# Hybrid block on one core: the state space group's tiles rebuilt, and linear attention's products issued in turn

## The chip, the core and the metric

One NeuronCore of a Trainium2 chip runs the kernel alone. The metric is the device time of one execution in microseconds; the figure given for a kernel is the median of several runs. TensorE multiplies on an array of 128 rows by 128 columns: a product's contraction lies on the rows (the partitions of its operands), its stationary operand's columns on the array's columns. The profile gives the clock that was granted to TensorE as a share of 2.4 GHz.

## The reference

A diffusion block on 1024 latent tokens behind 256 context tokens (D = 1024): one input projection feeds three groups (RWKV-7 with 4 heads, Mamba-2 state space with 8 heads of 64 and 2 groups of state 64, gated linear attention with 4 heads), an output projection joins them, and a mixture of experts follows. Each group is scanned in both directions and the two results are added. The state space group works in chunks of 128 tokens:

```python
def ssd_chunked(x, dA, bm, cm, s0):          # x is already times dt
    a_cs = cumsum(dA over the chunk)
    decay_in = exp(where(causal, a_cs[l] - a_cs[s], -inf))
    scores = einsum('bclhn,bcshn->bhcls', cm, bm) * decay_in
    y_diag = einsum('bhcls,bcshp->bclhp', scores, x)
    decay_to_end = exp(a_cs[-1] - a_cs)
    states = einsum('bclhn,bhcl,bclhp->bchpn', bm, decay_to_end, x)
    states = running sum over chunks, each decayed by the chunks behind it
    y_off = einsum('bclhn,bchpn,bhcl->bclhp', cm, states[:, :-1], exp(a_cs))
    return y_diag + y_off
```

Linear attention (`gla_chunked`) has the same form in chunks of 64 tokens with keys of 32 and values of 64: masked scores by values, and decayed queries by the chunk's state. (The code above is condensed.)

## The kernel before

The sequence is 10 tiles of 128 tokens; tiles 0 and 1 are context and give only states. `block_kernel` emits, in order: the input projection and the setup of all groups (to 560 us), 20 steps of the RWKV scan (`rw_step`), `rw_finish`, `gla_states`, `ssd_dt`, `ssd_states`, `ssd_out` for tiles 2 to 5, `gla_out`, the loads for the output projection, `ssd_out` for tiles 6 to 9, the output projection, routing, and the experts. This is not the order in which they run: the tile framework builds a timeline of its own from the emitted program and sets each engine's order from it, so the work of several of these functions is interleaved. Every engine then runs its list strictly in order; nearly all DMAs are issued on one queue, SP, in order too. PSUM is divided while the scan and the groups run: 2 buffers for the scan (`ch`), 1 (`rg`), 3 for the state space group (`sd`) and 2 for linear attention (`gl`).

The state space group before, per tile:

- `ssd_consts2` (L941) writes a template `difD` to DRAM early; `ssd_dt` (L955) fills it, by 32 small DMAs (L1015, L1016), with the cumulative sums of dA, each split into three bf16 parts so that bf16 products add up to float32 accuracy.
- `ssd_states` (L1019): the tile's x and B are transposed (`ptx`, `ptB`), x is multiplied by the decay to the chunk's end (`xs`, once per direction), and `pss` (L1044) gives the tile's state, [64 of a group's state rows on 64 partitions, 256]. Then, per direction, a chain on GpSimd over the tiles (`sacc`, L1059 multiply and L1061 add, 128x256), whose values ScalarE copies into `g.st` in SBUF.
- `ssd_weights` (L1067): `pe` (L1079), one bf16 product on 44 rows for each direction and half of the heads, gives the difference of cumulative sums at every (source, target); ScalarE copies one direction, VectorE takes the minimum of both, ScalarE the exponential (`E`). `pcb` (L1088) is C by B; VectorE multiplies it by the two masks (`M`), ScalarE and VectorE apply dt per head (`G`, L1094, L1095), GpSimd multiplies `E` by `G` (L1097).
- `ssd_out` (L1101): `pyo` (L1116) is C by the state, 64 rows and 512 columns; VectorE scales it (L1120), GpSimd adds the directions (`yo`); in `pyd`, x by `E` (L1131, two heads on the two column halves) and a transpose of `yo` by the identity (L1132) add up; VectorE adds the skip term (L1135), GpSimd gates (L1137), and squares are summed for the norm.

`gla_out` (L866): for each head `pat` (L880, 32 rows, 64 columns, the two chunks of a tile on the column halves) gives scores; `po` (L902, L905) collects values by scores and states by queries, one buffer after the other. `inv_norm` (L363) spreads norm factors over partitions with a float32 product by the identity (`pbn`, L378).

Of the kernel before, what the change touches and what calls it, by code (L numbers as in the profile page):

```python
# [362 lines left out]
def inv_norm(g, W, tag, sq, blk, scale, eps):  # L363
# [502 lines left out]
def gla_out(g):  # L866

    nc = g.nc
    W = g.gl
    for gr in range(2):  # L870
        att = W.tile([128, 2 * TT], F, tag="la", name="att", bufs=1)
        asum = att[:, 0:1024].rearrange("p (h j t) -> p h j t", h=4, j=4)
        for h in range(4):
            hs = slice(32 * h, 32 * h + 32)
            ps = g.ps.tile([128, 2, 4, 64], F, tag="gl", name="pat")
            for d in range(2):
                for j in range(4):
                    for i in range(2):
                        c = slice(512 * gr + 128 * j + 64 * i, 512 * gr + 128 * j + 64 * i + 64)
                        nc.tensor.matmul(ps[HS[i], d, j, :], g.gq[d][hs, 1, c], g.gq[d][hs, 0, c], start=True,  # L880
                                         stop=True)
            at = att[:, 1024 + 512 * (h % 2):1536 + 512 * (h % 2)].rearrange("p (d j t) -> p d j t", d=2, j=4)
            nc.gpsimd.memset(at, 0.0)
            for d in range(2):
                nc.vector.copy_predicated(at[:, d], g.mA[:, d, None, :].to_broadcast([128, 4, 64]), ps[:, d])
            nc.vector.tensor_add(asum[:, h], at[:, 0], at[:, 1])
        oTs = []
        for hp in range(2):
            oT = W.tile([128, 512], F, tag="oT", name="oT", bufs=2)
            for i in range(2):  # L890
                po = g.ps.tile([128, 4, 64], F, tag="gl", name="po")

                for d in (-1, 0, 1):
                    for j in range(4):
                        tl = 2 + 4 * gr + j
                        c = 2 * tl + i
                        cs = slice(64 * c - TC, 64 * c - TC + 64)
                        for h in (2 * hp, 2 * hp + 1):
                            o = po[HS[h % 2], j, :]
# [7 lines left out]
                nc.scalar.activation(oT.rearrange("p (j i t) -> p j i t", i=2, t=64)[:, :, i, :], po, AF.Copy)  # L907
# [32 lines left out]

def ssd_consts2(g):  # L941


    nc = g.nc
    g.difD = g.dram.tile([8, 44, 4, 5, 128], BF, name="difD")
    t = g.tmp.tile([44, 4, 5, 128], BF, tag="rv", name="dift", bufs=1)
    nc.gpsimd.memset(t, 0.0)
    nc.gpsimd.memset(t[0:12, :, 0], 1.0)
    for h in range(4):
        nc.sync.dma_start(t[32 + 3 * h:35 + 3 * h, :, 1 + h], g.oneb[0:3, None, :].to_broadcast([3, 4, 128]))  # L950
    nc.sync.dma_start(g.difD.rearrange("c p i j t -> p c (i j t)"),
                      t.rearrange("p i j t -> p (i j t)")[:, None].to_broadcast([44, 8, 2560]))


def ssd_dt(g):  # L955

    nc, W = g.nc, g.sd
    n = 160
# [14 lines left out]
    m = W.tile([128, 160], I32, tag="srs", name="dm")  # L973
    nc.vector.tensor_scalar(m, f(u), 1.0 / 16, None, op0=OP.is_lt)
    nc.vector.copy_predicated(f(e), m, f(p))
    nc.vector.tensor_scalar(x, x, 0.0, None, op0=OP.max)
    g.dtp = T("dtp")
    nc.vector.tensor_add(g.dtp, x, e)
    dA = T("dA")
    for d in range(2):  # L980
        nc.vector.tensor_mul(dA[:, d], g.dtp[:, d], g.nea[:, d, None, :].to_broadcast([128, 10, 8]))
    g.eacs, g.wend = T("eacs"), T("wend")
    tot = T("tot")
    for d in range(2):
        ps = g.ps.tile([128, 4, 128], F, tag="sd", name="psd")
        r = dA[:, d].rearrange("p c h -> p (c h)")
        nc.tensor.matmul(ps[:, 0, 0:80], g.mT[:, d, :], r, start=True, stop=True)
        nc.tensor.matmul(ps[:, 1, 0:80], g.mT[:, 2 + d, :], r, start=True, stop=True)
        nc.tensor.matmul(ps[:, 2, 0:80], g.onesm, r, start=True, stop=True)
        for i, dst in ((0, g.eacs), (1, g.wend), (2, tot)):  # L990
            nc.scalar.activation(dst[:, d].rearrange("p c h -> p (c h)"), ps[:, i, 0:80], AF.Exp)
    nc.vector.tensor_mul(g.wend, g.wend, g.dtp)

    g.dec = W.tile([128, 2, 10, 4], F, tag="dec", name="dec")
    for h in range(2):
        nc.vector.tensor_copy(g.dec[HS[h]], tot[HS[h], :, :, 4 * h:4 * h + 4])

    ps = g.ps.tile([128, 512], F, tag="sd", name="pcs")
# [12 lines left out]
    for d in range(2):
        for q in range(2):
            for h in range(4):
                src = parts[64 * d + 4 * q + h:64 * d + 64:8]
                nc.sync.dma_start(g.difD[:, 3 * h:3 * h + 3, 2 * d + q, 1 + h], src[:, 0:3])  # L1015
                nc.sync.dma_start(g.difD[:, 32 + 3 * h:35 + 3 * h, 2 * d + q, 0], src[:, 3:6])  # L1016


def ssd_states(g):  # L1019
    nc, W = g.nc, g.sd  # L1020
    g.xr = g.dram.tile([10, 128, 512], F, tag="sxr", name="sxr")
    g.st = W.tile([128, 2, 8, 256], F, tag="st", name="st")
    sc = W.tile([128, 2, 2, 256], F, tag="E", name="sc", bufs=2)
    for tl in range(10):
# [21 lines left out]
        nc.vector.tensor_copy(sc[:, :, tl, :] if tl < 2 else g.st[:, :, tl - 2, :], ps)

    for d in range(2):
        order = list(range(10)) if d == 0 else [1, 0] + list(range(9, 1, -1))
        acc = None  # L1050
        for i, tl in enumerate(order):
            own = sc[:, d, tl, :] if tl < 2 else g.st[:, d, tl - 2, :]
            if i == 0:
                acc = W.tile([128, 256], F, tag="sacc", name="sacc", bufs=3)
                nc.gpsimd.tensor_copy(acc, own)
                continue
            if i < 9:
                nxt = W.tile([128, 256], F, tag="sacc", name="sacc", bufs=3)
                nc.gpsimd.tensor_mul(nxt.rearrange("p (h c) -> p h c", h=4), acc.rearrange("p (h c) -> p h c", h=4),  # L1059
                                     g.dec[:, d, tl, :, None].to_broadcast([128, 4, 64]))  # L1060
# [753 lines left out]
```

## Time and profile before

| | |
|---|---|
| median of 3 runs | 1552.88 us (1551.18 to 1554.76) |
| profiled execution | 1557.75 us, its span 1555.9 us |
| mean granted clock | 0.874 |
| TensorE busy in the span | 1363.9 us (88%) |
| VectorE / ScalarE / GpSimd busy | 816.0 / 522.8 / 401.2 us |
| instructions | 28009 |

The span is the time between the first and the last record of the profiled execution; the rest of its time lies around it. A busy share over the whole span mixes stages that have different limits, so the stages are read apart: the projection to about 560 us, the RWKV scan to 730, what is left of the states to 780, the products of the state space group and of linear attention to 930, the output projection to 1057, routing to 1105, experts to the end. "Idle before" in a group names what the engine waited for last.

### The profile page before, as it was taken

What the parts mean: (1) busy time and instruction counts of PE and PEld (TensorE: products, weight loads), DVE (VectorE), ACT (ScalarE), POOL (GpSimd) and SP (SyncE); (2) the same over time, 40 slices, a digit from 0 to 9 for tenths busy, and PEclk for the clock granted to TensorE, in tenths of its full rate; (3) what the DMA queues carried; (4) which work ended last, traced back from release to release, by engine and by line L of the source; (5) the groups of instructions that cost most, each with busy time, mean ns of one, the idle gap of its engine ahead of it and who ended that gap; (6) DMA issues with size and microseconds to landing.
All of it is one profiled execution on the core that took longest, in us unless ns stands there. A gap on an engine that the chain in (4) does not pass through costs nothing. (4 is left out here: it accounts for less than half of the span.)

```text
span 1555.9 us, 28009 instructions
## 1 busy us (share of the span) xinstructions
PE 1363.9 (88%) x11016; PEld 1122.0 (72%) x11016; DVE 816.0 (52%) x1605; ACT 522.8 (34%) x1107; POOL 401.2 (26%) x447
## 2 busy tenths in 40 slices
PE   7897899999788777687899989993999999999985
PEld 2585677777677765576456857772999899899984
DVE  4849857889879754425753575326211312112532
ACT  5544334443263135423521443121311312212323
POOL 3312332343333112324722233112110211111111
PEclk9997799999899778799655559996999999999988
DMA  8455867676761475776322163434997978868984
GB/s 319 127 145 142 196 145 169 170 187 170 166 138 35 88 163 165 201 218 212 114 67 60 61 198 124 162 136 140 354 335 239 301 234 281 294 219 292 313 274 121
DMA packets 290244, 290.80 MB, mean 187 GB/s; under 512 B 112712, under 2 KB 211273, under 8 KB 290110
## 3 DMA queue, kind: packets, MB, share of 16 engines
q1 hardware_dynamic: 281086, 263.81, 55.7%
q0 software_dynamic: 7872, 20.97, 5.7%
q10 hardware_dynamic: 1152, 4.19, 0.7%
q8 instruction: 88, 1.44, 0.4%
q14 instruction: 46, 0.38, 0.1%
HBM read 217.96 MB, written 71.20 MB: 186 GB/s over the span
## 5 line engine op out<-in xcount | busy, mean ns | idle before, releaser
L1523 PE MATMUL p<-hT,w 128*128 128x144 f32 (+10 forms) x2048 | 261.7, 287 | 0.0
L1523 PEld LDWEIGHTS p<-hT,w 128*128 128x128 f32 x2048 | 256.2, 191 | 0.6
L262 PE MATMUL psi<-hlo,whi 128*128 128x512 f32 (+1 forms) x440 | 172.3, 392 | 5.1 <-DVE hlo L234 3.9
L261 PE MATMUL psi<-hhi,whi 128*128 128x512 f32 (+1 forms) x440 | 170.5, 389 | 0.0
L263 PE MATMUL psi<-hhi,wlo 128*128 128x512 f32 (+1 forms) x440 | 170.1, 387 | 0.3 <-POOL wlo L254 0.3
L1530 PE MATMUL p<-hid,w 128*128 128x144 f32 (+10 forms) x1024 | 133.7, 290 | 10.3 <-DVE hid L1525 9.1
L1530 PEld LDWEIGHTS p<-hid,w 128*128 128x128 f32 x1024 | 130.8, 194 | 11.0 <-DVE hid L1525 9.7
L1549 POOL DMA_INDIRECT acc<-yr,rows x27 | 41.4, 1532 | 319.5 <-DVE yr L1545 185.1
L1525 DVE TENSOR_TENSOR hid<-hid,p 128x144 f32<-128x144 f32 (+10 forms) x64 | 18.7, 293 | 177.6 <-PE p L1523 173.6
L262 PEld LDWEIGHTS psi<-hlo,whi 128*128 128x128 f32 x440 | 85.8, 195 | 26.2 <-DVE hlo L234 5.6
L263 PEld LDWEIGHTS psi<-hhi,wlo 128*128 128x128 f32 x440 | 85.5, 194 | 19.5 <-issue 3.7
L261 PEld LDWEIGHTS psi<-hhi,whi 128*128 128x128 f32 x440 | 85.7, 195 | 18.0 <-issue 2.4
L1545 DVE TENSOR_SCALAR yr<-pty,rows 128x512 f32<-128x512 f32 (+8 forms) x46 | 32.6, 740 | 101.3 <-PE pty L1539 101.3
L1531 ACT ACTIVATE yT<-p,mods 128x144 f32<-128x144 f32 (+10 forms) x128 | 42.7, 374 | 110.0 <-PE p L1530 109.9
L1524 ACT ACTIVATE hid<-p 128x144 f32<-128x144 f32 (+10 forms) x64 | 18.2, 284 | 164.0 <-PE p L1523 163.9
L740 DVE SCALAR_TENSOR_TENSOR co<-gr,pc,co 128x512 f32<-128x512 f32 x72 | 59.3, 849 | 5.8 <-ACT co L729 4.0
L190 DVE SCALAR_TENSOR_TENSOR aacc<-wada,csig,aacc 128x512 f32<-128x512 f32 x56 | 50.0, 893 | 10.4 <-DMA wada<-in_ada_w_dram 10.1
L261 PE MATMUL pso<-woh,mh 128*128 128x512 f32 x128 | 53.8, 425 | 0.8 <-ACT woh L1168 0.8
L262 PE MATMUL pso<-wol,mh 128*128 128x512 f32 x128 | 52.9, 413 | 0.2 <-DVE wol L1169 0.2
L263 PE MATMUL pso<-woh,ml 128*128 128x512 f32 x128 | 52.6, 411 | 0.0
L464 PE MATMUL psg<-AR,BK 64*128 64x128 f32 x320 | 46.6, 304 | 4.0 <-DVE BK L457 1.6
L1490 ACT ACTIVATE hT<-pte,mods,gs 128x128 f32<-128x128 f32 (+4 forms) x76 | 27.6, 446 | 66.7 <-PE pte L1486 66.7
(533 smaller groups left out, 2753.3 us busy)
## 6 DMA issues: line engine op xcount, KB each, us to landing
w<-in_moe_w_dram SPq DMA_DIRECT2D x47, 2048.0 KB
wada<-in_ada_w_dram SPq DMA_DIRECT2D x32, 512.0 KB
cd<-stepD SPq DMA_DIRECT2D x20, 768.0 KB
wraw<-in_w_in_dram SPq DMA_DIRECT2D x24, 512.0 KB
aw<-in_ada_w_dram SPq DMA_DIRECT2D x10, 512.0 KB
stepD<-AR SPq DMA_DIRECT2D x40, 128.0 KB
mabD<-G SPq DMA_DIRECT2D x40, 128.0 KB
stepD<-G SPq DMA_DIRECT2D x40, 128.0 KB
```

Of the source, the lines that this page charges most:

```text
L190: nc.vector.scalar_tensor_tensor(acc, w[:, k % 2], g.sg[:, k, 0:1], acc, op0=OP.mult, op1=OP.add)
L261: nc.tensor.matmul(ps, whi(k), xhi(k), start=k == 0, stop=False)
L262: nc.tensor.matmul(ps, whi(k), xlo(k), start=False, stop=False)
L263: nc.tensor.matmul(ps, wlo(k), xhi(k), start=False, stop=k == 7)
L464: nc.tensor.matmul(pg[h][:, c, :], bkf[HS[h], c], arf[HS[h], c], start=True, stop=True)
L740: nc.vector.scalar_tensor_tensor(o, src(dy, dx), w(3 * dy + dx), o, op0=OP.mult, op1=OP.add)
L1490: nc.scalar.activation(hT[:, k, c0:c0 + m], pt[:, j, 0:m], AF.Identity, scale=g.gs2[:, k:k + 1], bias=g.mods[:, 24 + k, 0:1])
L1523: nc.tensor.matmul(p[:, 0:n], w[:, k, fs], hT[:, k, s0:s0 + n], start=k == 0, stop=k == 7)
L1530: nc.tensor.matmul(p[:, 0:n], w2[:, f, 128 * k:128 * k + 128], hid[:, f, 0:n], start=f == 0, stop=f == 3)
L1531: nc.scalar.activation(yT[:, k, 0:n], p[:, 0:n], AF.Copy, scale=g.mods[:, 40 + k, 0:1])
L1545: nc.vector.tensor_scalar(yr[0:m, h], pf, wt[0:m, b:b + 1], None, op0=OP.mult)
L1549: nc.gpsimd.indirect_dma_start(out=g.acc, out_offset=bass.IndirectOffsetOnAxis(ap=rows[0:m, 0, b:b + 1], axis=0), in_=yr[0:m, :], in_offse ...
```

## The change

Four things. (1) The exponents of the state space weights are built whole by products: a mask of −1e38 by the identity, then two products on 36 rows (64 rows apart for the two halves of the heads) that add the differences of cumulative sums and the logarithm of dt; so ScalarE takes the exponential straight from PSUM, once per direction, and VectorE adds the directions and multiplies by C·B. (2) The state's share of the output is no longer a product of its own: `Cd`, C times the exponential of the cumulative sum for both directions (128 rows), enters the same sum in `pyd` as x by `E`, with the state as stationary operand; `pyo`, `yo` and the product by the identity go. (3) The states of both directions stand on the two partition halves of one sum `S[p]` (8 multiply and add pairs of 128x512); each sum is written to DRAM (`stD`) and read again per tile, and the tiles are visited in the order 0, 1, 2, 9, 3, 8, 4, 7, 5, 6. (4) `pat` and `po` are issued in turn over two heads or chunks, with both `gl` buffers in use, and `pbn` becomes a transpose.

```diff
@@ inv_norm
-        nc.tensor.matmul(pb[:, 128 * i:128 * i + 128],
-                         sq[:, 128 * i:128 * i + 128] if h > 1 else r[:, i:i + 1].to_broadcast([128, 128]), g.ident,
-                         start=True, stop=True)
+        nc.tensor.transpose(pb[:, 128 * i:128 * i + 128],
+                            sq[:, 128 * i:128 * i + 128] if h > 1 else r[:, i:i + 1].to_broadcast([128, 128]), g.ident)
@@ gla_out
-        for h in range(4):
-            hs = slice(32 * h, 32 * h + 32)
-            ps = g.ps.tile([128, 2, 4, 64], F, tag="gl", name="pat")
+        for hp in range(2):
+            pat = [g.ps.tile([128, 2, 4, 64], F, tag="gl", name="pat") for h in range(2)]
...
+                        for h in range(2):
+                            hs = slice(64 * hp + 32 * h, 64 * hp + 32 * h + 32)
+                            nc.tensor.matmul(pat[h][HS[i], d, j, :], g.gq[d][hs, 1, c], g.gq[d][hs, 0, c], start=True,
+                                             stop=True)
...
-            for i in range(2):
-                po = g.ps.tile([128, 4, 64], F, tag="gl", name="po")
+            po = [g.ps.tile([128, 4, 64], F, tag="gl", name="po") for i in range(2)]
@@ ssd_consts2
-    g.difD = g.dram.tile([8, 44, 4, 5, 128], BF, name="difD")
+    g.difD = g.dram.tile([8, 128, 8, 128], BF, name="difD")
...
+SORD = [0, 1, 2, 9, 3, 8, 4, 7, 5, 6]
@@ ssd_dt
+    nc.vector.tensor_scalar(p, dtp, 1.0e-18, None, op0=OP.max)
+    nc.scalar.activation(f(p), f(p), AF.Ln)
...
-                nc.sync.dma_start(g.difD[:, 3 * h:3 * h + 3, 2 * d + q, 1 + h], src[:, 0:3])
-                nc.sync.dma_start(g.difD[:, 32 + 3 * h:35 + 3 * h, 2 * d + q, 0], src[:, 3:6])
+                o = 64 * q + 3 * h
+                nc.sync.dma_start(g.difD[:, o + 12 * d:o + 12 * d + 3, h], src[:, 0])
+                nc.sync.dma_start(g.difD[:, o + 24:o + 27, 4 + d], src[:, 2])
+                nc.sync.dma_start(g.difD[:, o + 24:o + 27, 6 + d], src[:, 1])
@@ ssd_states
-                nc.gpsimd.tensor_mul(nxt.rearrange("p (h c) -> p h c", h=4), acc.rearrange("p (h c) -> p h c", h=4),
-                                     g.dec[:, d, tl, :, None].to_broadcast([128, 4, 64]))
-                nc.gpsimd.tensor_add(nxt, nxt, own)
-            if tl >= 2:
-                nc.scalar.activation(own, acc, AF.Copy)
+        while done < 9 and {(0, done), (1, done)} <= have:
+            p = done
+            if p:
+                t = W.tile([128, 8, 64], F, tag="st", name="sacc", bufs=2)
+                nc.gpsimd.tensor_mul(t, S[p - 1], g.dec[:, p, :, None].to_broadcast([128, 8, 64]))
+                nc.gpsimd.tensor_add(S[p], S[p], t)
+                nc.sync.dma_start(g.stD[p + 1], S[p].rearrange("p h c -> p (h c)"))
+            done += 1
@@ ssd_weights
-            nc.tensor.matmul(pe[d], df[:, 2 * d + q, 0], df[:, 2 * d + q, 1:5].rearrange("p h t -> p (h t)"), start=True,
-                             stop=True)
...
-        nc.vector.tensor_tensor(Eq, pe[1], Eq, op=OP.min)
-        nc.scalar.activation(Eq, Eq, AF.Exp)
...
-        for h in range(4):
-            dt = g.dtp[:, :, tl, 4 * gr + h:4 * gr + h + 1]
-            nc.scalar.activation(G[:, h], M[:, 1], AF.Copy, scale=dt[:, 1])
-            nc.vector.scalar_tensor_tensor(G[:, h], M[:, 0], dt[:, 0], G[:, h], op0=OP.mult, op1=OP.add)
...
-        nc.gpsimd.tensor_mul(Eg, Eg, G)
+    K = [slice(64 * q, 64 * q + 36) for q in range(2)]
+    R = [df[K[q], 0:4].rearrange("p h t -> p (h t)") for q in range(2)]
...
+        for q in range(2):
+            nc.tensor.matmul(pe[q], g.identb, g.negm[:, d, None, :].to_broadcast([128, 4, 128]), start=True, stop=False)
+        for q in range(2):
+            nc.tensor.matmul(pe[q].rearrange("p h t -> p (h t)"), df[K[q], 4 + d], R[q], start=False, stop=False)
+        for q in range(2):
+            nc.tensor.matmul(pe[q].rearrange("p h t -> p (h t)"), df[K[q], 6 + d], R[q], start=False, stop=True)
+        for q in range(2):
+            nc.scalar.activation(E2[q] if d else E[:, 4 * q:4 * q + 4], pe[q], AF.Exp)
...
+        nc.vector.tensor_add(Eq, Eq, E2[q])
...
+        nc.tensor.matmul(pa[q].rearrange("p h t -> p (h t)"), g.dirs[K[q]], R[q], start=True, stop=True)
...
+        nc.scalar.activation(Cd[:, h], pa[q], AF.Exp)
+        nc.gpsimd.tensor_mul(Cd[:, h], Cd[:, h], C2[:, q, None, :].to_broadcast([128, 4, 128]))
...
+        nc.vector.tensor_mul(Eg, Eg, pc[gr][:, None, :].to_broadcast([128, 4, 128]))
@@ ssd_out
-            nc.tensor.matmul(po.rearrange("p d h c -> p (d h c)"), xt[HS[gr], 5, :], g.st[HS[gr], :, tl - 2, :],
-                             start=True, stop=True)
...
-            nc.tensor.matmul(py[:, j, :], yo[:, 2 * j:2 * j + 2, :].rearrange("p h c -> p (h c)"), g.ident, start=False,
-                             stop=True)
+        st = W.tile([128, 8, 64], F, tag="st", name="st", bufs=2)
+        for d in range(2):
+            nc.sync.dma_start(st[HS[d]].rearrange("p h c -> p (h c)"), g.stD[spos(d, tl), HS[d]])
...
+            for i, (w, m) in enumerate(((x, E), (st, Cd))):
+                for h in range(2):
+                    nc.tensor.matmul(py[HS[h], j, :], w[:, 2 * j + h, :], m[:, 2 * j + h, :], start=i == 0, stop=i == 1)
```

The lists of the engines move with it. On SP in the RWKV scan, before: the last writes of `difD`, then `xt` for two tiles of states and a scan step's loads (`cd`, `sm`, `v`).

```order
L1015 DMA difD<-csp 8x3x128
L1016 DMA difD<-csp 8x3x128
L581 DMA cd<-stepD 128x1536
L1015 DMA difD<-csp 8x3x128
L1016 DMA difD<-csp 8x3x128
L1015 DMA difD<-csp 8x3x128
L1016 DMA difD<-csp 8x3x128
L583 DMA sm<-sD 128x2x128
L586 DMA sm<-mabD 128x2x64 x2
L1015 DMA difD<-csp 8x3x128
L1016 DMA difD<-csp 8x3x128
L1027 DMA xt<-xsD 128x5x128 x2
```

And after, at the same place, now three writes for each head; the first write of a state sum (`stD`) stands ahead of `xt`:

```order
L582 DMA sm<-sD 128x2x128
L585 DMA sm<-mabD 128x2x64 x2
L1058 DMA difD<-csp 8x3x128
L1056 DMA difD<-csp 8x3x128
L1057 DMA difD<-csp 8x3x128
L1058 DMA difD<-csp 8x3x128
L1111 DMA stD<-S_7502 128x512
L1074 DMA xt<-xsD 128x5x128 x2
L1123 DMA df<-difD 128x1024
L588 DMA v<-vtD 64x4x64 x2
```

The writes moved apart, over about six scan steps for two, and `xt` stands some five steps later. On SP behind the scan, after: the loads of a tile for `ssd_weights` (`xt_7902`, `df`, `C_7906`) stand among the writes of the state sums, each of which waits for a GpSimd add (before, no state was written).

```order
L1123 DMA df<-difD 128x1024
L1111 DMA stD<-S_7503 128x512
L1121 DMA xt_7902<-xsD 128x6x128
L659 DMA fw<-bvD 128x512
L660 DMA fw<-gtD 128x512
L1126 DMA C_7906<-xsD 64x2x128 x2
L1111 DMA stD<-S_7503 128x512
L1123 DMA df<-difD 128x1024
L1121 DMA xt_7980<-xsD 128x6x128
L1111 DMA stD<-S_7503 128x512
L1176 DMA st<-stD 64x512
```

On TensorE at the first tile of `ssd_out`, before (a float32 product counts once here):

```order
L1116 MATMUL pyo<-st,xt_7767 128x512 x2
L1131 MATMUL pyd<-E,x_7863 64x128 x2
L860 MATMUL pkv<-vg,ke 32x64 x4
L880 MATMUL pat<-gq_6909 64x64 x7
L1132 MATMUL pyd<-ident,yo 128x128
L1131 MATMUL pyd<-E,x_7863 64x128 x2
L1132 MATMUL pyd<-ident,yo 128x128
L1131 MATMUL pyd<-E,x_7863 64x128 x2
L1079 LDWEIGHTS df
L1079 MATMUL pe<-df 128x512
```

And after:

```order
L1188 MATMUL pyd<-E,x_7871 64x128 x2
L1135 LDWEIGHTS identb
L1135 MATMUL pe<-negm,identb 128x512
L1137 LDWEIGHTS df
L1137 MATMUL pe<-df 128x512
L1139 LDWEIGHTS df
L1139 MATMUL pe<-df 128x512
L370 MATMUL pin<-blk_91,fs 128x2 x4
L1135 LDWEIGHTS identb
L1135 MATMUL pe<-negm,identb 128x512
```

The products of `pe` now stand in threes, and those of two tiles and a half come ahead of the first `Cd` product, behind which `E` and `Cd` pairs alternate; all eight tiles stand ahead of the first product of the output projection (`pso`), where before the last two or three stood among them.

## Rows read from the trace of the kernel before

**Rows 1.** Windows: length; busy of PE, PEld, DVE, ACT, POOL; granted clock; DMA share; GB/s.

```profile
560.00:730.00 170.00, 127.39 (x2879) 105.27 (x2881) 67.81 (x147) 61.77 (x145) 48.19 (x51) 0.83 0.69 197
730.00:780.00 50.00, 37.38 (x275) 22.14 (x275) 40.49 (x82) 27.53 (x65) 35.53 (x38) 0.71 0.42 131
780.00:930.00 150.00, 142.05 (x981) 96.13 (x979) 77.59 (x193) 51.37 (x99) 39.42 (x37) 0.51 0.30 95
930.00:1057.00 127.00, 126.64 (x637) 93.85 (x636) 48.89 (x94) 34.74 (x62) 32.86 (x26) 0.99 0.40 136
```

**Rows 2.** Groups by line and form, TensorE, 730 to 930 us (busy us, mean ns).

```profile
L1116 PE MATMUL pyo<-st,xt 64*128 64x512 f32 x24 | 21.1, 1131 | 0.0
L1132 PE MATMUL pyd<-ident,yo 128*128 128x128 f32 x48 | 18.9, 498 | 0.0
L905 PE MATMUL po<-gq,gS 32*64 32x64 f32 x256 | 17.9, 315 | 0.0
L880 PE MATMUL pat<-gq 32*64 32x64 f32 x256 | 17.2, 316 | 0.0
L1079 PE MATMUL pe<-df 44*128 44x512 bf16 x30 | 15.6, 572 | 0.7 <-DVE yz L1135 0.7
```

**Rows 3.** Timeline of TensorE, 778 to 812 us (start, length, line, out<-in).

```profile
778.51 2.08 PE L1116 MATMUL pyo<-st,xt 64*128 64x512 f32 x4
...
795.35 2.07 PE L1116 MATMUL pyo<-st,xt 64*128 64x512 f32 x2
...
810.82 0.60 PE L1079 MATMUL pe<-df 44*128 44x512 bf16 x1
811.35 1.11 PE L905 MATMUL po<-gq,gS 32*64 32x64 f32 x14
```

**Rows 4.** Timeline of TensorE, pieces at 738, 825 and 865 us.

```profile
738.75 1.11 PE L1030 MATMUL ptx<-ident,xt 128*128 128x128 f32 x4
...
825.84 0.79 PE L1132 MATMUL pyd<-ident,yo 128*128 128x128 f32 x2
826.56 0.69 PE L1131 MATMUL pyd<-E,x 128*64 128x128 f32 x4
...
865.74 1.03 PE L1079 MATMUL pe<-df 44*128 44x512 bf16 x2
866.70 1.97 PE L880 MATMUL pat<-gq 32*64 32x64 f32 x32
```

**Rows 5.** Timeline of TensorE at 757, and windows with the granted clock.

```profile
756.97 2.07 PE L378 MATMUL pbn<-ident,fs 128*128 128x128 f32 x8
758.84 1.92 PE L663 MATMUL pm<-y,blk 128*128 128x512 f32 x2
...
760.00:762.00 2.00, 1.97 (x6) 0.67 (x5) 2.00 (x5) 1.60 (x5) 2.00 (x3) 0.72 0.02 7
762.00:764.00 2.00, 1.23 (x9) 1.04 (x9) 2.00 (x4) 1.36 (x4) 1.65 (x2) 1.00 0.70 182
786.00:928.00 142.00, 134.90 (x936) 92.17 (x936) 75.01 (x186) 49.99 (x97) 35.45 (x34) 0.50 0.30 92
```

**Rows 6.** Timeline of GpSimd, the last sum of the states.

```profile
776.13 0.90 POOL L1061 TENSOR_TENSOR sacc<-sacc,st 128x256 f32<-128x256 f32 x1
```

**Rows 7.** Line 1015 on SP (ns: least/median/most), and SP's timeline behind it.

```profile
L1015 SPq DMA_DIRECT2D difD<-csp x16: 567/567/673, 604.5 to 627.1; - x16
...
628.32 0.44 SPq L1027 DMA_DIRECT2D xt<-xsD  x1
```

**Rows 8.** Waits, TensorE 560 to 730 and SP 560 to 930 (total, times, longest).

```profile
PE ptx L1030 <- DMA xt<-xsD: 8.6, 1, 8.6
...
SPq L1111 <- DMA sxr<-x: 7.3, 2, 3.7
```

**Rows 9.** Groups by line and form, VectorE and GpSimd, 730 to 930 us.

```profile
L1095 DVE SCALAR_TENSOR_TENSOR G<-M,dtp,G 128x128 f32<-128x128 f32 x56 | 20.1, 405 | 2.9 <-ACT G L1094 2.8
...
L1097 POOL TENSOR_TENSOR E<-E,G 128x512 f32<-128x512 f32 x14 | 18.9, 1347 | 38.2 <-DVE G L1095 38.2
```

More of the change, by code (lines that the diff above doesn't have):

```diff
@@ L994, in ssd_dt @@
[L994 to L998, printed above, removed]
+    nc.vector.tensor_mul(g.wend, g.wend, dtp)
+    g.dec = W.tile([128, 10, 8], F, tag="dec", name="dec")
+    nc.vector.tensor_copy(g.dec[0:64], tot[0:64, 0])
+    nc.vector.tensor_copy(g.dec[64:128, 0:2], tot[64:128, 1, 1::-1])
+    nc.vector.tensor_copy(g.dec[64:128, 2:10], tot[64:128, 1, 9:1:-1])
@@ L1030, in ssd_states @@
             nc.tensor.transpose(pt[:, j, :], xt[:, j, :], g.ident)
+        pb = g.ps.tile([128, 512], F, tag="sd", name="ptB")
+        nc.tensor.transpose(pb[:, 0:128], xt[:, 4, :], g.ident)
         x = W.tile([128, 8, 64], F, tag="x", name="x", bufs=2)
@@ L1046, in ssd_states @@
[L1046 to L1058, printed above, removed]
-                nc.gpsimd.tensor_mul(nxt.rearrange("p (h c) -> p h c", h=4), acc.rearrange("p (h c) -> p h c", h=4),
-                                     g.dec[:, d, tl, :, None].to_broadcast([128, 4, 64]))
-                nc.gpsimd.tensor_add(nxt, nxt, own)
-            if tl >= 2:
-                nc.scalar.activation(own, acc, AF.Copy)
-            acc = nxt
+        ps = g.ps.tile([128, 8, 64], F, tag="sd", name="pss")
@@ new lines, in ssd_states @@
+        ds = [d for d in range(2) if spos(d, tl) < 9]
+        xs = {}
+        for d in ds:
+            xs[d] = W.tile([128, 8, 64], F, tag=f"xs{d}", name="xs", bufs=1)
+            (nc.gpsimd if d else nc.vector).tensor_mul(xs[d], x, g.wend[:, d, tl, :, None].to_broadcast([128, 8, 64]))
+        for gr in range(2):
+            for d in ds:
+                nc.tensor.matmul(ps[HS[d], 4 * gr:4 * gr + 4, :].rearrange("p h c -> p (h c)"), B[:, HS[gr]],
+                                 xs[d][:, 4 * gr:4 * gr + 4, :].rearrange("p h c -> p (h c)"), start=gr == 0,
+                                 stop=gr == 1)
@@ new lines, in ssd_states @@
+        for d in ds:
+            p = spos(d, tl)
+            have.add((d, p))
+            if d:
+                nc.vector.tensor_copy(S[p][HS[d]], ps[HS[d]])
+            else:
+                nc.scalar.activation(S[p][HS[d]], ps[HS[d]], AF.Copy)
+        while done < 9 and {(0, done), (1, done)} <= have:
[6 more added lines that the diff above has]
+            done += 1
@@ L1096, in ssd_weights @@
+    pc = [g.ps.tile([128, 128], F, tag="sd", name="pcb") for gr in range(2)]
+    for gr in range(2):
+        nc.tensor.matmul(pc[gr], xt[HS[gr], 4, :], xt[HS[gr], 5, :], start=True, stop=True)
+    for gr in range(2):
         Eg = E[:, 4 * gr:4 * gr + 4, :]
-        nc.gpsimd.tensor_mul(Eg, Eg, G)
-    return xt, E
+        nc.vector.tensor_mul(Eg, Eg, pc[gr][:, None, :].to_broadcast([128, 4, 128]))
+    return xt, E, Cd
 def ssd_out(g, tls):
@@ L1104, in ssd_out @@
     for tl in tls:
[L1105 removed]
+        xt, E, Cd = ahead
         if tl + 1 in tls:
             ahead = ssd_weights(g, tl + 1)
[L1108 removed]
+        zt = W.tile([128, 4, 128], F, tag="zt", name="zt", bufs=2)
         nc.sync.dma_start(zt, g.zsD[:, 0:4, 128 * tl:128 * tl + 128])
```

163 lines of the change are left out of this document (86 added, 77 removed).

## The prediction

> **What bounds the kernel now.** I read the windows by stage first [rows 1]. The change touches the four stages from 560 to 1057 us. In the 20-step scan (560 to 730) TensorE is busy 127.4 of 170 us and waits on transfers. Then 50 us pass in which no engine is full: TensorE 37.4, VectorE 40.5, GpSimd 35.5; the chain of state sums on GpSimd ends them, its last add runs from 776.1 to 777.0 [rows 6], and the first state product `pyo` starts at 778.5 [rows 3]. From 780 to 930 TensorE is the bound: 142.1 of 150 us busy at a granted clock of 0.51, which is the lower level, 1.2 GHz, while VectorE has half its time free. The output projection after it is dense, 126.6 of 127 us at 0.99. So from 780 to 930 a microsecond taken from VectorE, ScalarE or GpSimd is worth little; a microsecond of TensorE is worth nearly all of itself. That is the point on which this change must be weighed: it moves work from VectorE onto TensorE.
>
> What TensorE does there is in the groups by line [rows 2]. Neighbours overlap by some 0.07 us, so I price from start to start in the timeline where the next start is shown, else by the duration less that. One instruction costs at 1.2 GHz [rows 3, 4]: `ident` product 0.36 (two in 825.84 to 826.56); `E` product 0.16 (four in 0.69 less the overlap); `pat` 0.06 (32 in 1.97); `pe` 0.53 alone (810.82 to 811.35), and 0.43 for each that follows another (two last 1.03, one 0.60). A float32 product is two instructions, a bf16 product or a transpose one. A `pyo` product, two instructions, takes 2.0 us, but two of them on the two row halves, at 778.51, together take the same.
>
> **The change, part by part.**
>
> 1. Setup of `difD`, ahead of 100 us. Ten more small loads on SP and one input-projection weight block behind them; TensorE's stages up to 560 keep their order. Zero; if the cover is gone, some 6 us (ten issues of 0.57 [rows 7]).
>
> 2. The scan. The writes of `difD` go from 32 to 48. Each holds SP for 0.57 us [rows 7], so 16 more are +9 us of SP, in a place where SP is full: of before they stand from 604.5 to 627.7, the `xt` load of the third tile is issued behind them at 628.3, and TensorE waits 8.6 us for it between two scan steps [rows 7, 8]. In the order of after that tile's transposes stand about five steps later and the step loads stand between the writes, so that wait can vanish. I take +3; bounds −9 (wait gone, issues hidden) and +13 (all issues exposed and four state writes in the way).
>
> 3. The tail, 730 to 780. TensorE is idle 12.6 of 50 us [rows 1]. The sums become 8 multiply and add pairs of 128x512 in place of 18 pairs of 128x256, and VectorE loses the mask and dt products (the 56 `G` operations from 730 to 930 are 20.1 us [rows 9]), while TensorE has more `pe` products ready to fill gaps. I take −8 of the idle time, bounds −12.6 and 0. One more tile is left to do after the scan: five transposes of 0.26 (four `ptx` last 1.11 [rows 4]) and eight `pss` instructions, for which I take the same price, +3.
>
> 4. The SSD products of eight tiles. Out go `pyo`: 24 instructions, 21.1 us busy [rows 2], about 20 from start to start, and 8 more in the dense stage at half the price, −23 in all. Out go the `ident` products: 48 × 0.36 = 17.3 and 16 at half of it, −20. In come `pe` and `pa`: 14 per tile for 4, 80 more. In the order of after they stand mostly in threes and sixes, 80 × 0.45 = +36; bounds 80 × 0.43 = 34, and 42 at 0.53 each. In come `Cd` products, 128 instructions of the form of the `E` product: 128 × 0.16 = +20 if each costs as now, where the `E` fours stand between products of other forms; the lower bound prices `E` and `Cd` together as a run, each at twice a `pat` (128 columns for 64), 256 × 0.12 = 31 against 20 now, +11. I take +14. Sum −23 − 20 + 36 + 14 = **+7**, bounds +2 and +19. The gain on VectorE and ScalarE (no `G`, no minimum) is off the bound and counts nothing here.
>
> A rule of the Trainium skill, "TensorEngine Tiling (Array Packing)", section Key Properties, speaks against the change: changing the tiling mode drains the engine. Each `pe` of after goes from a 128-row product to products on 36 rows. By that rule, the single `pe` at 0.53 beside 0.43 in a pair [rows 3, 4] agrees in direction; with 0.53 for all of them the sum is 6 us worse.
>
> 5. Linear attention in turn. `pat` already runs at 0.06 per instruction, two column halves at a time. Whether four tiles do better isn't shown; at best the 256 `pat` and 256 `po` (17.2 and 17.9 us busy [rows 2]) halve, −17; at worst nothing. I take −6, as 0.05 for 0.06.
>
> 6. `pbn` as transposes: one instruction for two at 0.23 each (eight from 756.97 to 758.84 [rows 5]; the four `ptx` [rows 4] are nearly the same). 40 products × 0.23 = 9; a part of the `fs` ones lies in the tail's idle time. −7, bounds −9 and −4.
>
> 7. Idle in 780 to 930, 8 us [rows 1]: the chain from `pe` to the finished `E` loses eleven operations, −4 (−8 to 0).
>
> 8. The clock. It rises in the tail after 3.8 us of 128-row float32 products (`pbn` then `pm`, 756.97 to 760.76), from 0.72 in 760 to 762 to 1.00 after [rows 5]; TensorE's gaps then bring it back, and from 786 to 928 it is 0.50 throughout [rows 5] though TensorE hardly pauses. Runs of `pe` could raise it for short stretches. −4, bounds −10 and 0; a lasting rise is a rival.
>
> Sum: +3 − 8 + 3 + 7 − 6 − 7 − 4 − 4 = **−16 us**. The profiled run took 1557.75 us, of which the span is 1555.9; it is 0.3% above the median of 1552.88. From it the sum is 1541.8; from the median **1537 us**.
>
> **The rivals.**
>
> A: the clock stays up. Once TensorE streams `pe` runs and `pat` on several tiles without a gap, it may reach 2.4 GHz in the SSD stage and hold it until a gap. For it: the rise behind `pbn` and `pm` [rows 5]; against it: 142 us at 0.50 with TensorE busy for 134.9 of them. Half of the stage's 140 us at the upper level would halve that half, −35, less some 5 in which other engines then bind: 1537 − 30 = 1507.
>
> The Trainium skill, "TensorE: Matmul & The Clock Gate", Part 4: PE-mode transpose, says that transposes do not count for the clock as products do. By that rule `pbn` as transposes would weaken the rise after `pm`, and the tail stays at the lower level. The rows bear it out only so far: `ptx` runs in the tail [rows 4] are not followed by a rise.
>
> As a mechanism of this kernel, rival B: the rises of the tail are lost since `pbn` is half as long. About 12 of its 50 us run above 0.5 [rows 1]; at half speed that work takes 12 more, of which idle time takes a part: +7, and with `pe` at 0.53 each (+6) and no gain in 5 (+6) the sum is +3: 1552 to 1556. No change, or nearly.
>
> C: slower, by the queue of SP. The state sums are now written to DRAM and read back, and in the order of after the loads of the tiles' `xt`, `df` and `C` stand behind state writes that wait for a GpSimd add each; the tile that goes first needs the last sum. GpSimd has a multiply and an add of about 1.3 us each per sum (1.35 for `E` by `G`, 128x512 [rows 9]), mixed with `Cd`, `fw` and `kend`: four sums behind the last tile are 10 us, the rest of its queue as much again, then a write and a read through DRAM, some 3.5 us each (SP waits 3.7 for a tile just written [rows 8]). It is hidden as long as the last state is back by about 785, since TensorE has some 50 us of other work in its order. If GpSimd runs 20 us later, and the scan's loads lose the 13 us of step 2, it is −16 + 10 + 20 = +14: 1567.
>
> D: the change hardly moves the bound: `pe` products at their upper price cancel what 5 and 6 give, within B's range; counted there.
>
> **How the numbers follow.** Forecast without a lasting rise, 1537 (own range 1524 to 1550): 0.48. A: 0.26. B with D: 0.10. C: 0.16. The range must reach A's centre and C's beginning: 1500 to 1561. About 0.2%, 3 us, is what can be told from no change. Faster: A, nearly all of the forecast and a little of B, 0.74. Same: 0.09. Slower: C and a part of B, 0.17.
>
> **What would show it.** TensorE's busy time from the scan's end to the first `pso`: 179 us of before should stay about level at the lower clock. `ident` and `pyo` gone, 112 `pe` and `pa` at 0.43 to 0.53 us. VectorE's busy time there falls by a quarter or more; if the span falls with it while TensorE's does not, step 3 was too small. The granted clock of 780 to 930 above 0.6 is A. Long waits of `pyd` for `st` or `Cd`, or of SP for GpSimd ahead of `xt`, are C. Waits of the scan's `pa` for `cd` above the present ones are the upper bound of step 2. I would be wrong by most if the clock is not decided by what I read in rows 5.

## The result and the profile after

The changed kernel takes 1537.13 us (median of 4 runs, 1528.16 to 1548.77) against 1553.82 us of before (median of 4, 1551.18 to 1559.12): ratio 0.989, 95% interval 0.985 to 0.993. The profiled execution took 1533.99 us, 23.8 less than the profiled one of before. The median is the forecast to a tenth of a microsecond, which is luck with runs 20 us apart; the profile shows that it is put together otherwise.

The same four windows as in [rows 1]:

```profile
560.00:730.00 170.00, 127.56 (x2680) 104.85 (x2682) 64.44 (x146) 61.64 (x145) 42.03 (x43) 0.79 0.65 189
730.00:780.00 50.00, 45.05 (x454) 24.29 (x452) 32.25 (x56) 25.65 (x44) 29.35 (x23) 0.82 0.58 186
780.00:930.00 150.00, 135.92 (x1194) 99.29 (x1191) 76.40 (x137) 55.56 (x88) 53.32 (x51) 0.68 0.46 139
930.00:1057.00 127.00, 104.96 (x566) 80.53 (x564) 46.97 (x135) 26.61 (x47) 22.59 (x15) 0.92 0.42 146
```

The stages have shifted, so three milestones are safer: the scan's first and last `pa`, the last `pso`, the experts' first and last product. Their lines, before (least/median/most ns, first and last start):

```profile
L597 PE MATMUL pa<-v,cd x320: 217/218/365, 568.3 to 725.5; 64*64 64x64 f32 x160
...
L263 PE MATMUL pso<-woh,ml x128: 388/396/797, 920.9 to 1055.3; 128*128 128x512 f32 x128
...
L1523 PE MATMUL p<-hT,w x2048: 248/286/607, 1096.5 to 1528.3; 128*128 128x144 f32 x46, 128*128 128x96 f32 x24, 128*128 128x148 f32 x23, 128*128 128x192 f32 x12
```

and after:

```profile
L596 PE MATMUL pa<-v,cd x320: 218/218/367, 563.6 to 733.5; 64*64 64x64 f32 x160
...
L263 PE MATMUL pso<-woh,ml x128: 390/396/628, 906.2 to 1028.4; 128*128 128x512 f32 x128
...
L1576 PE MATMUL p<-hT,w x2048: 248/286/593, 1069.5 to 1504.4; 128*128 128x144 f32 x46, 128*128 128x96 f32 x24, 128*128 128x148 f32 x23, 128*128 128x192 f32 x12
```

| stage | before | after | difference |
|---|---|---|---|
| to the scan's first `pa` | 568.3 | 563.6 | −4.7 |
| scan, first to last `pa` | 157.2 | 169.9 | +12.7 |
| last `pa` to last `pso` | 329.8 | 294.9 | −34.9 |
| to the experts' first product | 41.2 | 41.1 | −0.1 |
| experts | 431.8 | 434.9 | +3.1 |

The first and the last row are no effect of the change: in the 14 traces of this study the first `pa` lies between 560.4 and 568.6 and the experts take 431.0 to 441.6, with no order by kernel. What the change did is +12.7 in the scan and −34.9 behind it.

**Behind the scan** the gain is the clock. Between the scan's last `py` and the last `pso` TensorE's busy time fell from 305.0 to 271.8 us and its idle time from 20.8 to 18.1, while the mean granted clock rose from 0.72 to 0.81. Busy time times clock, summed over windows of 2 us, is a rough measure of the work: 220.5 before, 217.8 after. Almost nothing of the work went away; it ran on the upper level for longer. At the clock of before, the work of after would have kept TensorE busy for some 301 us (305.0 × 217.8 / 220.5, an estimate), so about 29 of the 33 us by which its busy time fell are the clock's. It isn't one trace alone that shows this: in the four traces of kernels with the old tiles the mean clock of this stretch is 0.716 to 0.752, in the ten with the new ones 0.772 to 0.808. The trace shows where the clock rises, in a tile's uninterrupted run of `E` and `Cd` products (timeline of TensorE):

```profile
812.00 0.69 PE L1188 MATMUL pyd<-E,x 128*64 128x128 f32 x4
812.48 0.64 PE L1188 MATMUL pyd<-Cd,st 128*64 128x128 f32 x4
...
814.62 0.64 PE L1188 MATMUL pyd<-E,x 128*64 128x128 f32 x4
815.04 0.64 PE L1188 MATMUL pyd<-Cd,st 128*64 128x128 f32 x4
815.62 0.70 PE L1135 MATMUL pe<-negm,identb 128*128 128x512 bf16 x2
...
821.39 0.68 PE L907 MATMUL po<-gq,gS 32*64 32x64 f32 x16
822.00 0.48 PE L1156 MATMUL pcb<-xt 64*128 64x128 f32 x2
822.42 0.49 PE L907 MATMUL po<-gq,gS 32*64 32x64 f32 x6
822.84 0.79 PE L1156 MATMUL pcb<-xt 64*128 64x128 f32 x2
```

and the windows of 1 us around it (busy times by engine, then the granted clock):

```profile
814.00:815.00 1.00, 1.00 (x12) 1.00 (x11) 0.00 (x0) 0.00 (x0) 0.00 (x0) 0.50 0.18 49
815.00:816.00 1.00, 1.00 (x10) 0.41 (x6) 0.27 (x1) 0.00 (x0) 0.95 (x1) 0.58 0.00 0
816.00:817.00 1.00, 1.00 (x12) 0.33 (x12) 0.97 (x2) 0.11 (x1) 0.09 (x1) 1.00 0.68 141
821.00:822.00 1.00, 1.00 (x25) 0.85 (x25) 0.25 (x1) 0.61 (x2) 0.91 (x1) 1.00 0.00 0
822.00:823.00 1.00, 1.00 (x13) 0.76 (x9) 0.48 (x1) 0.00 (x0) 1.00 (x3) 0.83 0.68 186
823.00:824.00 1.00, 1.00 (x10) 0.78 (x11) 0.55 (x2) 0.00 (x0) 1.00 (x2) 0.50 0.20 76
```

Behind 3.6 us of `E` and `Cd` the clock goes to 1.00 at about 815.9, and in `po` and `pcb` products it falls back at 822.7 although TensorE is busy for all of that microsecond. All four rises between 780 and 906 us (815.9, 829.5, 877.3, 890.9) stand in or right behind such a run; in the trace of before, where `E` alternated with `ident` and other products stood between, that stretch had none until 928. The four runs of the changed kernel order by their mean clock: 0.894 for 1528.2 us, 0.890 for 1534.0, 0.887 for 1540.3, 0.881 for 1548.8.

**Prices at the lower level**, from the same timeline: single triples of `pe` take 0.50 per product, a triple of pairs 0.32, since two 36-row products on the two row halves run together (0.40 us for the pair at 865.60, 0.40 for the one at 867.11); `pat` is where it was.

```profile
842.37 1.97 PE L881 MATMUL pat<-gq 32*64 32x64 f32 x32
...
864.64 1.03 PE L1135 MATMUL pe<-negm,identb 128*128 128x512 bf16 x2
865.60 0.61 PE L1137 MATMUL pe<-df 36*128 36x512 bf16 x2
866.00 0.64 PE L1139 MATMUL pe<-df 36*128 36x512 bf16 x2
866.57 0.61 PE L1135 MATMUL pe<-negm,identb 128*128 128x512 bf16 x1
867.11 0.60 PE L1137 MATMUL pe<-df 36*128 36x512 bf16 x1
867.51 0.63 PE L1139 MATMUL pe<-df 36*128 36x512 bf16 x1
868.07 0.37 PE L370 MATMUL pin<-blk,gsq 128*128 128x2 f32 x1
```

**In the scan** TensorE waits longer for its step loads (waits of TensorE, 560 to 740; before, `pa` on `cd` was 7.2 us in three waits, and `ptx` on `xt` as in [rows 8]):

```profile
PE pa L596 <- DMA cd<-stepD: 13.9, 5, 5.0
...
PE ptx L1077 <- DMA xt<-xsD: 2.5, 1, 2.5
```

These two waits don't make up the 12.7 us, though: together they were 15.8 us and are 16.4. Of the scan from first to last `pa`, TensorE's idle time grew by 5.2 us (36.4 to 41.6) and its busy time by 7.5, at a clock of 0.80 for 0.83 and for no more work (busy time times clock 103.1 before, 101.1 after). Before, then after:

```profile
568.30:725.50 157.20, 120.77 (x2686) 99.32 (x2688) 57.26 (x130) 57.56 (x137) 43.74 (x48) 0.83 0.67 195
563.60:733.50 169.90, 128.28 (x2690) 105.56 (x2692) 62.69 (x143) 61.13 (x144) 43.21 (x44) 0.80 0.65 189
```

### The profile page after: what moved, and what is told of

Same layout as the page of the kernel before. It is cut to its first block, busy times and chain, and to the rows that moved or that the text cites. A ratio compares the mean times of both kernels' runs of the same rounds, so it can differ in the third digit from the quotient of the medians.

```text
span 1532.2 us, 28018 instructions
## 1 busy us (share of the span) xinstructions
PE 1340.5 (87%) x11077; PEld 1111.9 (73%) x11077; DVE 785.2 (51%) x1482; ACT 515.4 (34%) x1056; POOL 389.5 (25%) x432
## 5 line engine op out<-in xcount | busy, mean ns | idle before, releaser
L263 PE MATMUL psi<-hhi,wlo 128*128 128x512 f32 (+1 forms) x440 | 169.9, 387 | 0.3 <-POOL wlo L254 0.3
L1583 PEld LDWEIGHTS p<-hid,w 128*128 128x128 f32 x1024 | 133.9, 199 | 9.0 <-DVE hid L1578 7.5
L1578 DVE TENSOR_TENSOR hid<-hid,p 128x144 f32<-128x144 f32 (+10 forms) x64 | 18.7, 294 | 170.0 <-PE p L1576 165.9
L463 PEld LDWEIGHTS psg<-AR,BK 64*128 64x128 f32 x320 | 39.5, 204 | 13.4 <-issue 4.0
```

The lines of the kernel that those rows point to most:

```text
L263: nc.tensor.matmul(ps, wlo(k), xhi(k), start=False, stop=k == 7)
L463: nc.tensor.matmul(pg[h][:, c, :], bkf[HS[h], c], arf[HS[h], c], start=True, stop=True)
L1578: nc.vector.tensor_mul(hid[:, f, 0:n], hid[:, f, 0:n], p3[:, 0:n])
L1583: nc.tensor.matmul(p[:, 0:n], w2[:, f, 128 * k:128 * k + 128], hid[:, f, 0:n], start=f == 0, stop=f == 3)
```

## The experiments

Two theories of the gain: the **work theory** of the prediction (each edit takes or adds TensorE time) and the **clock theory** (long runs of `E` and `Cd` raise the clock). One of the loss: the **SP theory** (16 more writes among the scan's loads). Ratios are to the kernel before on the same chip and in the same runs, with 95% intervals.

**Linear attention in turn.** `gla_out` of before in the changed kernel, and later in the faster kernel with 12 copies (below):

```diff
-        for hp in range(2):
-            pat = [g.ps.tile([128, 2, 4, 64], F, tag="gl", name="pat") for h in range(2)]
+        for h in range(4):
+            hs = slice(32 * h, 32 * h + 32)
+            ps = g.ps.tile([128, 2, 4, 64], F, tag="gl", name="pat")
...
```

> The changed kernel with linear attention's products back in the order of before (one head or chunk after the other, one buffer at a time). Work theory (the prediction's step 5): 6 us slower than the changed kernel, about 1543. Clock theory (the gain is a higher granted clock from 780 to 905 us, brought by the long runs of E and Cd products; in the trace of the changed kernel 32 pat still take 1.97 us, as before): no difference from the order itself, 1537 within 5, and pat again 1.97 for 32 at the lower clock.

1543.12 us, 0.9926 (0.9898 to 0.9953): intervals that touch those of the changed kernel.

> The kernel with 12 copies for difD, and linear attention's products back in the order of before. The first undoing gave 6 us with intervals that touch. If in turn is worth something (step 5, 6 us): 1531 or more. If it is worth nothing (32 pat took 1.97 us in either order): 1525 within 3.

1528.96 us, 0.9821 (0.9790 to 0.9851), the same as that kernel with the products in turn (0.9818). 32 `pat` take 1.97 us in both. Turn by turn over two heads is worth nothing that can be measured; the first 6 us were not repeated.

**`pbn` as a float32 product again**, in the changed kernel and in the one with 12 copies, and **as a transpose alone** in the kernel before:

```diff
-        nc.tensor.transpose(pb[:, 128 * i:128 * i + 128], sq[...], g.ident)
+        nc.tensor.matmul(pb[:, 128 * i:128 * i + 128], sq[...], g.ident, start=True, stop=True)
```

> The changed kernel with pbn as a float32 product by the identity again. Work theory (step 6): 40 more instructions of 0.23 us, of which a part lies in idle time, 7 us slower, about 1544. Clock theory: what is lost in work can come back where pbn's longer stretch raises the clock earlier, 1537 to 1541.

1550.67 us, 0.9988 (0.9965 to 1.0011), 15 us worse than 0.989 by the ratios and twice what step 6 says; why it is twice isn't shown.

> The kernel with 12 copies for difD, and pbn as a float32 product again. Work theory (step 6): 7 us slower, 1532. If the 13 us that the same edit cost the changed kernel hold everywhere: 1538. If pbn's worth hangs on the order around it (8 us lost where it was changed alone in the kernel before): anything, and the granted clock from the scan's end to the first pyd tells: above 0.66 with the longer pbn.

1536.15 us, 0.9873 (0.9842 to 0.9905) against 0.9818: 8.5 us worse, near the size of step 6, with intervals that touch. The clock from the scan's end to the first `pyd` is 0.69 against 0.66, so the higher clock that the longer `pbn` was expected to bring came too, and didn't pay for it.

> The kernel before with nothing changed but pbn as a transpose. The prediction's step 6: 7 us faster, 1546. From the run with pbn undone (13 us slower than the changed kernel): 12 or more, 1541 or less. If transposes count less for the clock: the rises behind pm in the tail (730 to 780 us) are gone and the gain is below 4 us.

1559.12 us, 1.0045 (1.0019 to 1.0070): alone, the transposes make the kernel before slower, by 7 us. The window 730 to 780 shows a part of it (compare [rows 1]: 37.38 busy at 0.71):

```profile
730.00:780.00 50.00, 35.12 (x275) 20.31 (x274) 37.76 (x77) 28.81 (x65) 33.53 (x37) 0.61 0.37 119
```

Of the three rises of before in that stretch (747, 761 and 771), the two behind `pbn` and `pm` are gone. That is rival B's mechanism, at half of its price: from the last `py` to the first `pyd` it is 54.8 us against 51.0. Where the 7 us lie isn't shown: from there to the last `pso` this trace is 5.3 us shorter than that of before, and the experts, which the edit doesn't touch, are 4.6 longer. The Trainium skill, "TensorE: Matmul & The Clock Gate", Part 4: PE-mode transpose, says that a transpose doesn't count for the clock as a product does; this trace agrees, 0.61 against 0.71, though a shorter stretch alone could do the same, which was not told apart. In the changed kernel the transposes pay; that this is so because `pe` products fill the stretch there was not tested.

**The writes of `difD`.** First both `pe` difference products joined into one on 48 rows, with 32 or 48 writes (in both the exponents come out otherwise than in the changed kernel, so they serve for the price of products and writes alone):

```diff
-                nc.sync.dma_start(g.difD[:, o + 24:o + 27, 4 + d], src[:, 2])
-                nc.sync.dma_start(g.difD[:, o + 24:o + 27, 6 + d], src[:, 1])
+                e = 64 * q + 24 + 6 * h
+                nc.sync.dma_start(g.difD[:, e:e + 6, 4 + d], src[:, 1:3].rearrange("p g r t -> p (g r) t"))
...
-            nc.tensor.matmul(pe[q].rearrange("p h t -> p (h t)"), df[K[q], 6 + d], R[q], start=False, stop=True)
```

> The changed kernel with both difference products of a (direction, half) joined into one on 48 rows (the logarithm of dt on 12 rows of its own), so 32 bf16 products fewer, and with 32 writes of difD in place of 48 (the two parts that stand in neighbouring rows go in one). SP theory (the scan is 12.6 us longer than before because 16 more writes of 0.57 us stand between its loads): scan 6 to 9 us shorter than the changed kernel's 169.9. Products: 32 x 0.2 to 0.43, 6 to 12 us less TensorE time at the lower clock. Together 1520 to 1526. If the writes are not what slows the scan: 1528, scan 168 to 171.

1517.64 us, 0.9763 (0.9727 to 0.9799).

> As the one before, with the joined products but 48 writes of difD. SP theory: the scan stays at about 170 us, 1528. If the writes do not matter: the same time as the kernel with 32 writes.

1531.14 us, 0.9857 (0.9834 to 0.9880). The joined products are worth some 5 us (0.9857 against 0.989, intervals that touch), the 16 writes 13.5 us; in the two traces the scan is 5.5 us longer with them (169.4 against 163.9). Then the kernel before with 16 of its writes issued twice:

```diff
                 nc.sync.dma_start(g.difD[:, 32 + 3 * h:35 + 3 * h, 2 * d + q, 0], src[:, 3:6])
+                nc.sync.dma_start(g.difD[:, 32 + 3 * h:35 + 3 * h, 2 * d + q, 0], src[:, 3:6])
```

> The kernel before with each of the 16 writes of the negated parts of difD (L1016) issued twice, so 48 writes in place of 32; nothing else. SP theory: 16 x 0.57 to 0.61 us of SP stand in front of the scan's loads, 8 to 13 us slower than before, 1559 to 1565, the scan 168 to 174 in place of 161, waits of pa for cd above 12 us. If the longer scan of the changed kernel came from its other work (states, sums): 1551 to 1554.

1575.32 us, 1.0111 (1.0079 to 1.0143): 17 us slower, more than expected. Its scan is 166.7 us from first to last `pa` (157.2 before), and its waits (560 to 745):

```profile
PE pa L597 <- DMA cd<-stepD: 16.0, 8, 3.2
PE ptx L1031 <- DMA xt<-xsD: 13.0, 1, 13.0
```

8.8 us more for `cd` and 4.4 more for `xt`; the scan is 9.5 us longer, and the rest of the 17 us isn't located. Last, the changed kernel with 12 copies:

```diff
+    nc.sync.dma_start(csD, parts)
     for d in range(2):
         for q in range(2):
-            for h in range(4):
-                src = parts[64 * d + 4 * q + h:64 * d + 64:8]
...
+            src = csD[64 * d:64 * d + 64].rearrange("(c h) k i t -> c h k (i t)", h=8)[:, 4 * q:4 * q + 4]
+            o = 64 * q
+            nc.sync.dma_start(dap(g.difD, (o + 12 * d) * 128, [[131072, 8], [16768, 4], [1, 384]]), src[:, :, 0])
+            nc.sync.dma_start(g.difD[:, 4 + d, o + 24:o + 36].rearrange("c (h r) t -> c h (r t)", h=4), src[:, :, 2])
+            nc.sync.dma_start(g.difD[:, 6 + d, o + 24:o + 36].rearrange("c (h r) t -> c h (r t)", h=4), src[:, :, 1])
```

> The changed kernel with both difference products, but difD is filled by one write of all parts to DRAM and 12 copies from there (three for each direction and half), in place of 48 writes; its rows are laid out slot by slot, so each tile's df load has pieces of 256 bytes. SP theory (the 16 more writes among the scan's loads cost the change 8 to 14 us): the waits of pa for cd fall from 13.9 to 7 us or less, the scan from 174.9 to at most 168, the time to 1520 to 1527. If the small pieces of the df loads hold TensorE up: waits of pe for df, 1530 to 1540.

1525.49 us, 0.9818 (0.9783 to 0.9853), some 11 us faster than the changed kernel and the fastest here with the exponents of the changed kernel. Its line of `pa`:

```profile
L596 PE MATMUL pa<-v,cd x320: 213/218/366, 560.4 to 721.0; 64*64 64x64 f32 x160
```

The scan is back at 160.6 us. The waits for `cd` fell only to 11.0 us (six, none over 2.6), not to the 7 expected, and that sum is a poor sign of the writes: it is 11.0 to 14.9 us in the four traces with 12 copies, 5.7 to 12.3 in the four with 32 writes and 13.9 to 17.9 in the six with 48. The length of the scan is the better one: over all traces it takes 166.7 to 175.8 us with 48 writes and 155.8 to 165.9 with 32 or 12, whichever the rest of the kernel. TensorE's idle time in the scan goes with it: 48 writes for 32 add 7.7 us (joined products) and 11.9 (kernel before), 12 copies for 48 writes take 6.4 away. So of the 12.7 us by which the change lengthened the scan the 16 writes are some 5.5 to 9.5, by these traces, and 3.4 stay even with 12 copies.

**The runs.** The changed kernel without its `Cd` products, and the kernel before with every `E` product twice:

```diff
-            for i, (w, m) in enumerate(((x, E), (st, Cd))):
+            for i, (w, m) in enumerate(((x, E),)):
...
```

> The changed kernel without the 64 Cd products (the state's share is missing from the output; all else, loads and the making of Cd too, stays). Work theory: 128 instructions of 0.107 us at the lower clock go, 14 us faster than the changed kernel, 1523, at the same granted clock. Clock theory (uninterrupted runs of 32 E and Cd instructions, 3.4 us, raise the clock): with runs of 16 the clock rises less often, its mean from the first to the last pyd falls from 0.65 to below 0.6, and the gain is eaten: 1532 to 1545.

1533.66 us, 0.9879 (0.9851 to 0.9906), hardly faster than the changed kernel, though 128 of the 1115 instructions between its first and last `pyd` are gone. From first to last `pyd`:

```profile
781.60:892.40 110.80, 105.53 (x962) 70.45 (x963) 59.19 (x100) 48.37 (x76) 40.90 (x42) 0.57 0.44 128
```

0.57 against 0.65, as the clock theory has it. But this stretch did get shorter by what the work theory says, 110.8 us for 125.3; the gain is lost behind it. From the last `pyd` to the last `pso`, without `Cd` and then in the changed kernel:

```profile
892.40:1027.50 135.10, 128.48 (x602) 98.49 (x601) 44.13 (x84) 35.65 (x56) 30.68 (x23) 0.92 0.44 152
905.00:1028.40 123.40, 119.16 (x580) 91.31 (x577) 37.48 (x65) 30.89 (x51) 30.34 (x22) 0.97 0.41 140
```

That is 11.7 us longer: without `Cd` the output projection starts at the lower level, which lasts from 896.3 to 916.8, where in the changed kernel the rise at 890.9 holds until 911.

> The kernel before with every E product issued twice into the same sum (the diagonal share of the state space output counts double; 64 more products). Work theory: 128 instructions of 0.107 to 0.16 us, 14 to 20 us slower than before, 1567 to 1573, clock from 780 to 930 still 0.5. Clock theory: denser work on the whole array raises the clock there above 0.55, and less than 8 us are lost.

1575.87 us, 1.0133 (1.0089 to 1.0177), by the ratio 21 us slower, of which the trace has 15.0 between the scan's last `py` and the last `pso`: here the clock theory missed. The doubled products do not form runs, since `ident` products and others still stand between them; two short rises come (777 and 893 us), the rest stays at 0.50 (0.55 in the mean from 780 to 930). So more dense work is not enough. Nor does a rise need `Cd`: without it there are still two in the stage and one right behind it (865.6, 879.2, 892.9), and in the kernel before with doubled writes, whose TensorE work is that of before, the clock rises at 800.7, behind `E`, `pbn` and `ident` products and one short row of `pkv` (timeline, then windows):

```profile
797.17 0.69 PE L1132 MATMUL pyd<-E,x 128*64 128x128 f32 x4
797.80 0.47 PE L860 MATMUL pkv<-vg,ke 64*32 64x64 f32 x16
798.19 2.07 PE L378 MATMUL pbn<-ident,fs 128*128 128x128 f32 x8
800.06 0.64 PE L1133 MATMUL pyd<-ident,yo 128*128 128x128 f32 x2
...
800.00:801.00 1.00, 1.00 (x8) 0.61 (x6) 0.88 (x2) 0.00 (x0) 0.42 (x1) 0.65 0.00 0
801.00:802.00 1.00, 1.00 (x9) 0.64 (x7) 0.55 (x1) 0.00 (x0) 0.35 (x1) 1.00 0.00 0
```

Products of 128 rows stand ahead of these rises, in the changed kernel without interruption, in others with short 36-row or 64-row products between (865.6, 777). No run varied the length of such a run alone, so which streams raise the clock is read from the lists and not shown by an experiment.

The last, with each tile's `E` products ahead of all its `Cd` products:

> The kernel with 12 copies for difD, and in each tile all E products ahead of all Cd products (the same sum), so that a tile's E products need not wait for its states. Work theory: nothing, or up to 3 us less waiting, 1522 to 1526. Clock theory: the run of a tile stays as long, so the same clock and 1522 to 1528; if E products are drawn ahead and the runs break, the clock falls and it is slower, 1530.

1529.24 us, 0.9824 (0.9788 to 0.9859): no difference; the runs stay as long.

## Why the prediction was right, and where its steps were not

The number, the sign and the range held. The sum did not: errors of both signs cancelled, so the total was right by luck.

| step | forecast | shown |
|---|---|---|
| 1 setup | 0 | not told from the spread of the scan's start |
| 2 scan | +3 | +12.7, near its upper bound |
| 3 tail | −8 + 3 | last `py` to first `pyd` 51.0 to 41.2 us; idle 12.6 to 4.0 |
| 4 products | +7 | about 0 by the lower-level prices |
| 5 in turn | −6 | 0 |
| 6 `pbn` | −7 | −8.5 and −15 undone, but +7 alone |
| 7 idle | −4 | +2 (8.1 to 9.9 us from first to last `pyd`) |
| 8 clock | −4 | most of the 34.9 us (some 29 by the estimate above) |

- **Step 2** failed by size. I hid two thirds of the 16 writes behind the `xt` wait that vanishes. It did shrink (8.6 to 2.5 us), but the waits for `cd` grew by as much (7.2 to 13.9), and the sum had no term for the clock in the scan: 7.5 of the 12.7 us are busy time at a lower level. Sixteen writes alone lengthened the scan by 5.5 and 9.5 us in the two pairs of traces whose edits differ in nothing else, where I took 3 of their 9.
- **Step 3** came out: idle time fell by 8.6 us for the 8 forecast. But 4.2 us of idle time came in behind the last `pyd`, where before had none, and no step has that.
- **Step 4**: `pe` came near its price (0.50 alone, 0.32 in pairs, for 0.45). `E` and `Cd` in a run cost 0.107 us each (four from 812.48 to 812.91), below the lower bound, so 256 of them are 27 us against 20, +7 and not +14.
- **Step 5** failed: I took −6 though no row showed four tiles doing better than two column halves, and they don't: 1.97 us for 32 `pat` in either order.
- **Step 6** had the right size here, and the wrong independence: the same edit costs 7 us in the kernel before. Rival B, which had this, misread [rows 1]: 0.71 over 50 us is some 21 us at the upper level, not 12, of which 7 (to 737) are left from the scan.
- **Step 8** is the step that failed most. The mark that I set for rival A, a clock above 0.6 from 780 to 930, was passed: 0.65 between first and last `pyd`. Rival A's mechanism happened in good part and for a reason it half named (it had `pe` runs and `pat`; in the trace the rises stand in runs of `E` and `Cd`, and the clock falls in `po` and `pcb`). That 1537 came out and not 1507 is owed in part to steps 2, 5 and 7. I had also read that only TensorE's gaps bring the clock back; 822.7 shows a fall without one.
- **Rival C** named SP, and the scan's part of it came (12.7 us for 13); its main part did not: behind the scan `pyd` waits for `st` only 1.8 us.
- **The signs.** TensorE's busy time from the scan's last `py` to the first `pso` did not stay level: 168.1 us before (the 179 of the prediction runs to 930) and 153.3 after, at 0.68 for 0.56. VectorE's fell by 13% (108.9 to 94.3), not by a quarter.

How much of the 34.9 us is clock and how much work isn't settled to better than some 5 us, since a product at the upper level takes a little over half of its time at the lower (four `E` in a run 0.22 us at 829.53, 0.43 at 812.48).

## What to carry to other kernels

Price an edit of TensorE's order by what it does to the clock, too: which products stand without interruption, and which streams let the level fall. Count a row of small DMAs by the queue that they stand in: 16 writes of 0.57 us among the loads of a scan made two kernels 13 and 17 us slower, 5.5 and 9.5 of it in the scan itself, and gathering them into a few copies gave 11 us back. A forecast that comes true should still be taken apart by its terms, since one total cannot tell a good sum from a lucky one.

## What was not expected of the hardware

The granted clock falls to the lower level under a TensorE that is busy for every microsecond, in products of 32 and 64 rows (822 to 824 us), and rises behind 3.6 us of products on 128 rows in two column halves (815.9). Replacing float32 products by transposes, half as many instructions, made a kernel 7 us slower, with the clock from 730 to 780 us at 0.61 for 0.71; that the 7 us lie there isn't shown.
